# Two pairs of experts summed in PSUM before one eviction, with gather and sum moved around the transposes

## The chip, the cores and the metric

One core of a Trainium2 chip runs the whole program as a single launch. The metric is the device time in microseconds (us) of that launch; less is better. The core has TensorE (PE, with its weight loads PEld), VectorE (DVE), ScalarE (ACT), GpSimd (POOL) and the queue of SyncE (SP), from which most transfers out of device memory are issued. Each engine works through its own instructions in a fixed order and waits on semaphores for the others.

## What is computed

Two transformer blocks on 256 tokens of width 1024. The change lies in the second block, which has two layers. Each layer ends with a mixture of experts: 32 experts in 4 groups, of which every token uses the best two of its best group. In layer 0 there are 512 tokens (256 of the sequence and 256 of a context), in layer 1 only the 256 of the sequence. In short:

```python
def hier_moe(x, ...):
    g_idx = argmax(x @ w_group + b_group)            # group of a token, g_w its probability
    top_l, top_i = top_k(logits of that group, 2)
    top_w = softmax(top_l) * g_w
    expert = g_idx * 8 + top_i
    # every expert on the tokens that chose it
    hdn = silu(xb @ w_gate[e]) * (xb @ w_up[e])      # [n, 1024] -> [n, 512]
    ys = hdn @ w_down[e]                             # [n, 512] -> [n, 1024]
    return sum over a token's two experts of ys * top_w
h = h + gt2 * hier_moe(modulate(rms_norm(h)))
```

All inputs are float32. The weights of the 32 experts are 201 MB per layer (three matrices of 2 MiB per expert) and are read once.

## The kernel before

Everything of interest is in `moe(l, row, rt)`, which is run once per layer. Its slots give each expert 64 places for tokens (a rare expert with more tokens is treated after the loop). The loop `for P in range(16)` goes over pairs of experts, 2P and 2P + 1; four experts, so two pairs, are a quad `qd`.

- **Products of a pair.** `ex` computes gate, up and down for both experts of a pair side by side: expert i has 64 columns of the array, so that two matmuls of 64 columns run at the same time. Gate and up are 16 matmuls each (8 chunks of 128 features, 2 experts), down 16 (4 chunks, 2 halves of the output, 2 experts). They are float32, and each shows as two records in the trace. `next_tile` brings the weights in tiles of 1 MiB in the order of use, 12 per pair. The tiles go round seven places (four `raw`, three made of a `hi` and a `lo` buffer); six more tiles per layer, `early`, `rows` and `gt`, wait in other places from before the loop. So 13 tiles are loaded ahead, and later tiles are issued from SP as places come free.
- **Gather.** `gather(qd, kks)` fills `xq`, the features of the 4 x 64 slots of a quad, by matmuls with one-hot rows `oh` (line 1503), at 128 x 256. In layer 0 there are 64 per quad and half of them stand in each pair of the quad before. The one-hots are made by DVE inside `gather` (lines 1486 to 1493), at the place where the first half of the gather stands.
- **Combine.** `slots(P)` makes the one-hot `oht` and the weights of a pair on DVE. `y` is the pair's weighted output, split in two float32r parts by ACT (line 1600) and DVE (line 1601). `combine` turns it back to tokens: for each tile t of 128 tokens and each half n of the features, which I call a unit, two matmuls (line 1542) go into a PSUM buffer `tp`, DVE multiplies by the gate into `res` (line 1544, the eviction), and POOL adds `res` to `h` (line 1546; in the last pair DVE). Layer 0 has 8 units per pair, layer 1 has 4. There are three `tp` buffers, shared by gather, transposes and combine.
- **Transposes.** `sl = silu(gate) * up` (line 1572 on ACT, line 1578 on DVE) is transposed by four matmuls (line 1587), copied by ACT to `hT` (line 1589), and down follows.

In the text the combine of pair P - 1 stands around the product up of pair P, the gather ahead of the transposes. That is not the order on an engine: a scheduler at build time lays out each engine's instructions, by its own estimates, and may put them earlier. On PE, matmuls of combine are woven between those of gate and up.

Of the kernel before, what the change touches and what calls it, by code (L numbers as in the profile page):

```python
# [7 lines left out]
F32 = mybir.dt.float32  # L8
# [8 lines left out]
D = 1024  # L17
# [8 lines left out]
# ---------------------------------------------------------------------------  # L26
# constants that depend on shapes alone, packed in one [128, *] float32 array
# ---------------------------------------------------------------------------
# [10 lines left out]
def build_consts():  # L39
# [36 lines left out]
    # relative bias of the dilated mixer: bucket one-hot over m = t - s + 127  # L76
# [17 lines left out]
# units of background work (the modulation of the second block) emitted in the phases of the first block  # L94
# [6 lines left out]
def build(nc, tc, I, O, stop=""):  # L101
    """I: dict of input APs, O: output AP [256, 1024]."""
# [10 lines left out]
    @contextmanager  # L113
    def phase(name, nblk, nsm, nrow=1, nraw=0, ring=0):
        """Work memory of one phase: nblk blocks of 8 KB per partition, nsm of 2 KB, nrow of 4 KB; nraw more raw
        weight tiles; ring: further places in the order of the weight tiles."""
        with tc.tile_pool(name=name, bufs=1, reuse_waits="tile") as p:
            cur.update(pool=p, nblk=nblk, nsm=nsm, nrow=nrow, nraw=nraw, ring=ring, i=0)
            yield p
# [3 lines left out]
    def fill(n=1):  # L123
        """Emits n units of the background generators."""
        while n and bg:
            if next(bg[0], bg) is bg:
                bg.pop(0)
            else:
                n -= 1

    class Weave:
        """Spreads the units of generators over the slots of another loop."""
# [17 lines left out]
    def pipelined(n, stages, between=None):  # L150
        """stages[j](i) for items i < n, stage j of an item j steps after its first."""
# [11 lines left out]
    def blk(shape, dt=F32, name="blk", glob=False):  # L163
        """A block of the phase, or one that outlives it."""
# [84 lines left out]
    def load_exp(ap):  # L249
        """4 (or 2) k chunks of an expert's weight, also in buffers of split weights; k -> [128, width]."""  # L250
# [14 lines left out]
    class W:  # L265
        """Rows chunks of a weight tile as pairs (hi, lo)."""
# [29 lines left out]
    def rsqrt(ssq, n, inv_d):  # L296
        """(ssq * inv_d + eps) ** -0.5 for [128, n] sums of squares."""
# [12 lines left out]
    def rsqrt2(s0, s1, inv_d):  # L310
        """((s0 + s1) * inv_d + eps) ** -0.5 for two [128, 1] partial sums of squares."""
# [20 lines left out]
    def to_fm(src, nk, nt, xh, xl, gain=None, k0=0):  # L332
        """TM [128, nt, nk * 128] -> FM float32r pairs xh, xl [128, nk, nt * 128]; gain(k) -> [128, 1] column."""
# [22 lines left out]
    def row_rstd(hv, scr):  # L356
        """rms norm factor of the tokens of hv [128, D]; scr is overwritten."""
# [5 lines left out]
    def norm_tm(h, nt, rowv=None, glob=True):  # L363
        """h * rstd per token (* rowv), TM."""
# [28 lines left out]
    def token_order(kq, nt):  # L393
        """Order of (k, token tile) of a quad of k chunks: the last quad token by token."""
# [4 lines left out]
    class OutProj:  # L399
        """h += rms_norm(x @ w) * g; wtile(j) -> split pair [128, 2, 1024] of two k chunks."""  # L400
# [10 lines left out]
        def upto(self, xs, j1):  # L411
            """The k chunks below 2 * j1, the last pair of all token by token."""
# [30 lines left out]
    # ======================= first block =======================  # L443
    late = {}

    def rope_tables():
        SP.dma_start(consts[:, 128:], I["consts"][:, 128:CSPLIT])
        # rope tables of the positions: cos, sin [128, 2, 16]
# [29 lines left out]
    def setup():  # L478
        # conditions: silu(c), silu(c_ctx) as columns 4, 5; 32 columns from 4 - 2 c on have them at 2 c, 2 c + 1
# [11 lines left out]
        # lambda of both layers, on every partition  # L491
# [20 lines left out]
        # neighbourhood bias, rows (query row, head, key row), columns 63 - (kc - qc), in DRAM scratch  # L512
# [13 lines left out]
    def mla_layer():  # L526
        j = 0
        with phase("mla", 7, 7) as mp:
# [12 lines left out]
            # low-rank norms  # L541
# [27 lines left out]
            # q, TM, with rope on the last 32 of each 96  # L569
# [25 lines left out]
            # k (nope | rope) and v, TM  # L595
# [94 lines left out]
    def dil_bias():  # L690
        """Bias of the dilated heads over m = t - s + 127, to a DRAM scratch [48, 512]; loads first."""
# [14 lines left out]
    def dil_layer():  # L706
        with phase("dil", 5, 5) as mp:
# [8 lines left out]
            for qd in range(4):  # L716
# [24 lines left out]
                for hh in range(4):  # L741
# [3 lines left out]
                    # keys run backwards along the tile  # L745
# [47 lines left out]
    def ffn_layer(l):  # L793
        with phase(f"ffn{l}", 6, 8):
# [33 lines left out]
            # p @ ple_w_proj  # L828
# [33 lines left out]
    # ======================= second block =======================  # L862
# [5 lines left out]
    class Ada:  # L868
        """m = cond @ w_ada + b, row 32 j + 2 c + cond of [128, 512] for block 4 c + j, and as columns."""
# [32 lines left out]
        def cols(self, i):  # L902
            """[128, j2, b, cond] of parameter i."""
# [3 lines left out]
        def row(self, dst, i, cnd, n0, n1):  # L907
            """Halves n0 to n1 of parameter i on every partition."""
# [4 lines left out]
    def mixer(l, ada):  # L913
# [5 lines left out]
        # modulation columns g * (1 + scale), shift: [128, j2, b, cond]  # L919
# [7 lines left out]
        # x = modulate(rms_norm(h)), FM pairs, 4 k chunks of 512 tokens per block  # L927
# [24 lines left out]
        def proj_fm(c0, ntok, evac):  # L952
            """4 chunks of 128 columns from c0, FM over ntok tokens; evac(chunk, psum)."""
# [11 lines left out]
        def proj_tm(c0, ntile, evac):  # L965
            """512 columns from c0, TM; evac(t, psum)."""
# [28 lines left out]
        def transposed(p_sb, n, name):  # L995
            """[128 q, n * 128] -> [128 k, n * 128] blocks."""
# [13 lines left out]
        # keys, values, queries of the neighbourhood attention; halves of the spatial gating  # L1010
# [15 lines left out]
        def keys(t):  # L1026
            """First key and number of keys of a query tile."""
# [733 lines left out]
```

## Time and profile before

| | |
|---|---|
| timed runs | 3035.09, 3041.41, 3043.16 us, median 3041.41 |
| profiled execution | span 3046.4 us from the first to the last instruction; no other time is listed for it |
| PE busy | 2842.3 us, 93% of the span |
| DVE, ACT, POOL busy | 1383.3, 946.0, 384.1 us (45%, 31%, 13%) |
| transfers | 702.36 MB, on average 231 GB/s |
| expert loop of layer 0 (first product to last down) | 1599.7 to 2150.5 us |
| expert loop of layer 1 | 2548.1 to 3028.0 us |

The shares are averages over a program of many stages. PE is the busiest engine, but a PE that is "busy" may be at half clock, and the two expert loops have different limits, so they are read apart, by windows. In the timeline, rows of the same kind that follow one another are merged; the first number is the start, the second the length, and the bracket at the end is idle time with the engine that ended it. Matmuls overlap, so what one costs is read from start to start.

### The profile page before, as it was taken

Reading aid. Unit: us, or ns where it says so; the run is one execution under the profiler, and the core shown is the slowest. Engines: PE = TensorE matmul, PEld = TensorE weight load, DVE = VectorE, ACT = ScalarE, POOL = GpSimd, SP = SyncE. Lnnn points to the kernel's source line nnn. Section 1 sums busy time; section 2 is a strip of 40 time slices with the busy share of each in tenths; the row PEclk is TensorE's granted clock in tenths of the full one; section 3 lists DMA queues with packets and bytes.
Section 4 is the critical chain, followed back from the end, with each engine's and each line's share of the span. In section 5 each row is a group of like instructions: output and inputs, shape, how many; then the busy total and the mean of one; then the engine's idle time right before and its main releaser. Section 6 shows DMA issues by size and latency. Waiting matters only on the chain. (4 is left out here: it accounts for less than half of the span.)

```text
span 3046.4 us, 39455 instructions
## 1 busy us (share of the span) xinstructions
PE 2842.3 (93%) x15583; PEld 1972.6 (65%) x15583; DVE 1383.3 (45%) x2942; ACT 946.0 (31%) x1630; POOL 384.1 (13%) x304
## 2 busy tenths in 40 slices
PE   7999999998999999999979999999799997999996
PEld 6699789886997786678764444443486894333332
DVE  6555555445555426533472333333537564222222
ACT  5444444333444333433331001010334442111111
POOL 1010000000000201101031322223201001111111
PEclk9999999999999999999989999999899998999999
DMA  6665665665656432113468889889432386999997
GB/s 201 232 204 189 213 207 155 193 201 180 197 184 221 154 93 47 59 49 97 141 228 327 347 347 359 331 346 395 143 125 69 123 278 253 409 398 409 409 409 300
DMA packets 317148, 702.36 MB, mean 231 GB/s; under 512 B 36055, under 2 KB 179694, under 8 KB 310686
## 3 DMA queue, kind: packets, MB, share of 16 engines
q1 hardware_dynamic: 316622, 698.20, 64.0%
q8 instruction: 125, 2.05, 0.3%
q10 hardware_dynamic: 336, 1.59, 0.1%
q14 instruction: 65, 0.53, 0.0%
HBM read 697.91 MB, written 1.81 MB: 230 GB/s over the span
## 5 line engine op out<-in xcount | busy, mean ns | idle before, releaser
L280 DVE TENSOR_TENSOR lo<-raw,hi 128x1024 fp32r<-128x1024 f32 (+1 forms) x404 | 500.7, 1240 | 573.3 <-ACT hi L279 572.4
L279 ACT CAST hi<-raw 128x1024 fp32r<-128x1024 f32 (+1 forms) x418 | 433.7, 1039 | 623.4 <-PE mm L292 341.9
L291 PE MATMUL mm<-xh,hi 128*128 128x256 f32 (+1 forms) x1728 | 544.2, 316 | 3.7 <-ACT hi L279 2.5
L292 PE MATMUL mm<-xl,hi 128*128 128x256 f32 (+1 forms) x1728 | 538.3, 312 | 0.5 <-DVE xl L944 0.5
L293 PE MATMUL mm<-xh,lo 128*128 128x256 f32 (+1 forms) x1728 | 535.2, 310 | 1.2 <-POOL lo L280 1.2
L291 PEld LDWEIGHTS mm<-xh,hi 128*128 128x128 f32 x1728 | 333.4, 193 | 45.1 <-issue 20.3
L1532 PE MATMUL mm<-raw,xq 128*64 128x512 f32 x1152 | 345.3, 608 | 7.1 <-DMA raw<-in_moe_w_up_dram 3.9
L293 PEld LDWEIGHTS mm<-xh,lo 128*128 128x128 f32 x1728 | 333.0, 193 | 18.4 <-issue 1.8
L292 PEld LDWEIGHTS mm<-xl,hi 128*128 128x128 f32 x1728 | 333.5, 193 | 17.5 <-issue 2.0
L1546 POOL TENSOR_TENSOR h<-h,res 128x512 f32<-128x512 f32 x120 | 150.2, 1273 | 758.0 <-DVE res L1544 713.5
L1544 DVE TENSOR_TENSOR res<-tp,gt 128x512 f32<-128x512 f32 x192 | 123.0, 684 | 235.7 <-PE tp L1542 235.7
L1532 PEld LDWEIGHTS mm<-raw,xq 128*64 128x64 f32 x1152 | 100.0, 139 | 175.5 <-issue 156.6
L1601 DVE SCALAR_TENSOR_TENSOR y<-mm,wsum,y 128x512 fp32r<-128x512 f32 x64 | 47.1, 749 | 306.0 <-ACT y L1600 304.0
L291 PE MATMUL mm<-hi,xh 128*128 128x512 f32 (+2 forms) x504 | 174.9, 349 | 0.0
L293 PE MATMUL mm<-hi,xl 128*128 128x512 f32 (+2 forms) x504 | 174.9, 347 | 0.0
L292 PE MATMUL mm<-lo,xh 128*128 128x512 f32 (+2 forms) x504 | 174.4, 346 | 0.0
L1532 PE MATMUL mm<-raw,hT 128*64 128x512 f32 x568 | 160.1, 597 | 12.8 <-ACT hT L1589 12.6
L1532 PE MATMUL mm<-hi,xq 128*64 128x512 f32 x428 | 167.4, 603 | 0.6 <-DMA hi<-in_moe_w_up_dram 0.6
L1532 PE MATMUL mm<-lo,xq 128*64 128x512 f32 x428 | 159.7, 593 | 0.0
L1505 ACT COPY xq<-tp 128x512 f32<-128x512 f32 x64 | 37.5, 587 | 348.6 <-PE tp L1503 348.6
L280 POOL TENSOR_TENSOR lo<-raw,hi 128x1024 fp32r<-128x1024 f32 x14 | 33.7, 2422 | 861.2 <-ACT hi L279 766.0
L1542 PEld LDWEIGHTS tp<-y,oht 128*128 128x128 f32 x384 | 63.7, 188 | 119.3 <-issue 47.9
(486 smaller groups left out, 4588.3 us busy)
## 6 DMA issues: line engine op xcount, KB each, us to landing
raw<-in_moe_w_gate_dram SPq DMA_DIRECT2D x77, 1024.0 KB
raw<-in_moe_w_down_dram SPq DMA_DIRECT2D x71, 1024.0 KB
raw<-in_moe_w_up_dram SPq DMA_DIRECT2D x67, 1024.0 KB
raw<-in_w_in_dram SPq DMA_DIRECT2D x56, 1024.0 KB
raw<-in_w_ada_dram SPq DMA_DIRECT2D x48, 1024.0 KB
raw<-in_ffn_w_in_dram SPq DMA_DIRECT2D x44, 1024.0 KB
raw<-in_dil_w_qkv_dram SPq DMA_DIRECT2D x36, 1024.0 KB
hi<-in_moe_w_up_dram SPq DMA_DIRECT2D x59, 512.0 KB
```

What stands on the lines that cost most here:

```text
L279: A.copy(hv, rv[:, k0:k0 + n, :])
L280: (eng or V).tensor_tensor(lv, rv[:, k0:k0 + n, :], hv.bitcast(F32), op=ALU.subtract)
L291: T.matmul(ps, lhsT=lh, rhs=rh, start=first, stop=False)
L292: T.matmul(ps, lhsT=lh, rhs=rl, start=False, stop=False)
L293: T.matmul(ps, lhsT=ll, rhs=rh, start=False, stop=last)
L1505: A.copy(xq[:, 2 * kk:2 * kk + 2, :], p.rearrange("p (a b) -> p a b", b=256))
L1532: T.matmul(p[n][64 * i:64 * i + 64, :], lhsT=lhs(k, i), rhs=rv[i][kk][:, n * 512:(n + 1) * 512], start=k == 0, stop=k == kn - 1)
L1542: T.matmul(p, lhsT=oht[:, t * 128:(t + 1) * 128], rhs=y[:, i, ns], start=i == 0, stop=i == 1)
L1544: V.tensor_tensor(tmp, p, gts[:, t // 2, ns], op=ALU.mult)
L1546: (G if P < 15 else V).tensor_tensor(hs, hs, tmp, op=ALU.add)
L1601: V.scalar_tensor_tensor(y[:, 1, ns], py[n], wsum, y[:, 0, ns].bitcast(F32), op0=ALU.mult, op1=ALU.subtract)
```

## The change

- The one-hots of the gather get a function of their own, `onehots(qd)`, called in the even pair of a quad behind `slots`, instead of inside `gather`.
- `gather(qd + 1, ...)` moves wholly into the odd pair: two of its four parts ahead of the transposes, two behind them (between the transposes and down).
- `combine` now takes a list of two pairs (`done`), and sums four matmuls into one PSUM buffer per unit. It stands in the even pair alone: five eighths of the units ahead of the transposes, the rest behind them.
- `oht` of `slots` lies in a block of its own with four places, `ohts`, instead of one of the 2 KB buffers.
- In the last pair (P = 15), four units of the quad's first pair are begun before down, in three `tp` buffers and `po`; after the loop they are finished with the second pair's two matmuls, and other units get four matmuls in `mm` buffers. DVE adds these to `h`.

The core of the diff (comments and moved slices left out; line numbers of the changed file are about 20 to 40 higher, combine's matmul is line 1544, its eviction 1550, the gather's matmul 1505, products 1534, transposes 1604):

```diff
+        def onehots(qd):
+            dq = tiny.tile([128, nt, 2], F32, tag=f"dq{nt}", name="dq")
+            ...
+            state[qd] = (blk([128, 8, 256], name="xq", glob=True), oh)
         def gather(qd, kks):
-            if 0 in kks:
-                dq = tiny.tile([128, nt, 2], F32, tag=f"dq{nt}", name="dq")
-                ...
-                state[qd] = (blk([128, 8, 256], name="xq", glob=True), oh)
             xq, oh = state[qd]
 ...
-            oht = small(NT, F32R, name="oht")
+            oht = ohts[:, P % 4, :NT]
 ...
+        def summed(p, parts, t, n, first, last):
+            for j, (oht, y) in enumerate(parts):
+                for i in range(2):
+                    T.matmul(p, lhsT=oht[:, t * 128:(t + 1) * 128], rhs=y[:, i, ws_[n]], start=first and j + i == 0,
+                             stop=last and i == 1 and j == len(parts) - 1)
+        def added(p, t, n, eng):
+            tmp = small(name="res")
+            V.tensor_tensor(tmp, p, gts[:, t // 2, ws_[n]], op=ALU.mult)
+            hs = ht(t)[:, ws_[n]]
+            eng.tensor_tensor(hs, hs, tmp, op=ALU.add)
+        def combine(parts, us):
+            for t, n in us:
+                p = ps_tp()
+                summed(p, parts, t, n, True, True)
+                added(p, t, n, G)
 ...
             if P:
                 oht, wsum = slots(P)
-            if prev:
-                combine(*prev, range(nt // 2))
+            if not odd and qd < 7:
+                onehots(qd + 1)
             ex([pu], 8, xcols, 512)
             V.tensor_tensor(sl, sl, pu, op=ALU.mult)
 ...
-            if prev:
-                combine(*prev, range(nt // 2, nt))
-            if qd < 7:
-                gather(qd + 1, (0, 1) if P % 2 == 0 else (2, 3))
+            if odd:
+                if qd < 7:
+                    gather(qd + 1, (0, 1))
+            elif done:
+                combine(done, units[:cut])
             p = ps_tp()
             for b in range(4):
                 T.transpose(p[:, b * 128:(b + 1) * 128], sl[:, b * 128:(b + 1) * 128], ident)
             hT = small(name="hT")
             A.copy(hT, p)
+            if odd:
+                if qd < 7:
+                    gather(qd + 1, (2, 3))
+                else:
+                    for j, (t, n) in enumerate(units[:4]):
+                        open_.append(ps_tp() if j < 3 else ps_po())
+                        summed(open_[-1], now, t, n, True, False)
+            elif done:
+                combine(done, units[cut:])
             py = [ps_mm(), ps_mm()]
             ex(py, 4, lambda k, i: hT[:, k * 128 + i * 64:k * 128 + i * 64 + 64], 1024)
 ...
-            prev = (P, oht, y)
-        combine(*prev, range(nt))
+            now.append((oht, y))
+            if odd:
+                done, now = now, []
+        for j, (t, n) in enumerate(units):
+            if j < 4:
+                summed(open_[j], done[1:], t, n, False, True)
+                added(open_[j], t, n, V)
+            else:
+                p = ps_mm()
+                summed(p, done, t, n, True, True)
+                added(p, t, n, V)
```

What the scheduler makes of it is seen at three places of layer 0. In these rows `xq` stands for products gate and up, `hT` for down, `y,oht` (later `y,ohts`) for combine, `oh` for gather, and `consts,silu` for the transposes; what comes ahead of an arrow's comma list as `raw`, `hi` or `lo` is the weight tile.

DVE in the even pair P = 2, from the pair's `oht` on. Before:

```order
L1518 SCALAR_TENSOR_TENSOR oht<-rows,sid,o1t 128x512
L1544 TENSOR_TENSOR res<-tp,gt_13680 128x512 x4
L1510 TENSOR_SCALAR sid<-consts 128x1
L1578 TENSOR_TENSOR silu<-silu,mm 128x512
L1544 TENSOR_TENSOR res<-tp,gt_13680 128x512 x4
L1492 TENSOR_SCALAR o_14334<-consts,dq 128x256
L1492 TENSOR_SCALAR o_14337<-consts,dq 128x256
L1493 SCALAR_TENSOR_TENSOR oh<-consts,dq,o_14334 128x256
L1493 SCALAR_TENSOR_TENSOR oh<-consts,dq,o_14337 128x256
```

After:

```order
L1520 SCALAR_TENSOR_TENSOR ohts<-rows,sid,o1t 128x512
L1492 SCALAR_TENSOR_TENSOR oh<-consts,dq,o_14212 128x256
L1491 TENSOR_SCALAR o_14215<-consts,dq 128x256
L1491 TENSOR_SCALAR o_14218<-consts,dq 128x256
L1492 SCALAR_TENSOR_TENSOR oh<-consts,dq,o_14215 128x256
L1492 SCALAR_TENSOR_TENSOR oh<-consts,dq,o_14218 128x256
L1550 TENSOR_TENSOR res<-tp,gt_13680 128x512 x3
```

The one-hots stood behind the eight evictions of the pair; now they stand in front of all of them.

PE in pair P = 4, from its first combine to its transposes. Before (these rows are followed by the last six products and by 32 matmuls of the gather):

```order
L1542 MATMUL tp<-y,oht 128x512 x6
L1532 MATMUL mm<-raw,xq 64x512 x16
L1532 MATMUL mm<-hi,xq 64x512 x4
L1532 MATMUL mm<-lo,xq 64x512
L1542 MATMUL tp<-y,oht 128x512 x2
L1532 MATMUL mm<-lo,xq 64x512 x3
L1542 MATMUL tp<-y,oht 128x512
L1532 MATMUL mm<-hi,xq 64x512
L1542 MATMUL tp<-y,oht 128x512 x7
L1532 MATMUL mm<-raw,xq 64x512
```

After:

```order
L1544 MATMUL tp<-y,ohts 128x512 x4
L1534 MATMUL mm<-raw,xq 64x512
L1544 MATMUL tp<-y,ohts 128x512 x8
L1534 MATMUL mm<-raw,xq 64x512 x15
L1534 MATMUL mm<-hi,xq 64x512 x4
L1534 MATMUL mm<-lo,xq 64x512 x4
L1534 MATMUL mm<-hi,xq 64x512
L1544 MATMUL tp<-y,ohts 128x512 x8
```

The combine of the even pair now goes over two pairs, in fewer and longer runs; there is still a run of one matmul of the products (the second row).

PE around the transposes. Before (P = 4), they come behind the gather and directly before down:

```order
L1503 MATMUL tp<-oh,xlo 128x256
L1503 MATMUL tp<-oh,xhi 128x256
L1503 MATMUL tp<-oh,xlo 128x256
L1503 MATMUL tp<-oh,xhi 128x256
L1503 MATMUL tp<-oh,xlo 128x256
L1587 MATMUL tp<-consts,silu 128x128 x4
L1532 MATMUL mm<-raw,hT 64x512 x9
```

After (P = 4):

```order
L1534 MATMUL mm<-raw,xq 64x512
L1534 MATMUL mm<-lo,xq 64x512
L1534 MATMUL mm<-raw,xq 64x512
L1534 MATMUL mm<-lo,xq 64x512
L1534 MATMUL mm<-raw,xq 64x512
L1604 MATMUL tp<-consts,silu 128x128 x4
L1544 MATMUL tp<-y,ohts 128x512 x12
L1534 MATMUL mm<-raw,hT 64x512 x9
```

Now the last product of up stands directly before the transposes, and combine (in odd pairs gather) between the transposes and down.

## Rows read from the trace of the kernel before

**Rows 1.** Windows of the two expert loops; the first line names the columns

```profile
core 0: us, PE busy (x) PEld busy (x) DVE busy (x) ACT busy (x) POOL busy (x), PEclk, DMA share, GB/s
...
1599.70:2150.50 550.80, 514.78 (x2289) 222.27 (x2288) 182.13 (x349) 56.83 (x94) 150.49 (x120) 0.98 0.89 345
...
2548.10:3028.00 479.90, 443.73 (x1945) 172.87 (x1944) 115.58 (x258) 57.63 (x94) 75.10 (x60) 1.00 0.99 392
```

**Rows 2.** Waits of PE in layer 0's loop: us in total, times, longest us

```profile
PE tp L1503 <- DVE oh L1493: 16.8, 8, 4.7
PE mm L1532 <- ACT hT L1589: 12.6, 16, 1.1
PE tp L1542 <- ACT y L1600: 3.2, 4, 0.8
PE tp L1587 <- DVE silu L1578: 1.7, 2, 0.9
PE tp L1542 <- DVE y L1601: 1.4, 5, 0.3
```

**Rows 3.** Waits of PE in layer 1's loop

```profile
PE tp L1587 <- DVE silu L1578: 8.8, 11, 0.9
...
PE mm L1532 <- DMA raw<-in_moe_w_up_dram: 3.9, 5, 1.5
PE mm L1532 <- DMA raw<-in_moe_w_gate_dram: 3.2, 3, 1.5
```

**Rows 4.** Window inside layer 1's loop

```profile
2725.00:2750.00 25.00, 23.42 (x106) 8.91 (x108) 5.57 (x10) 2.36 (x4) 5.01 (x4) 1.00 1.03 409
```

**Rows 5.** Timeline of DVE, end of the even pair P = 8

```profile
1893.57 2.32 DVE L1492 TENSOR_SCALAR o<-consts,dq 128x256 f32<-128x256 f32 x2
```

**Rows 6.** Windows of layer 0's loop at half clock: one of five, and their sum

```profile
1820.10:1826.90 6.80, 6.02 (x14) 2.00 (x15) 2.44 (x7) 0.00 (x0) 0.18 (x1) 0.50 0.55 218
...
sum 27.20, PE 24.34 PEld 16.19 DVE 10.35 ACT 0.53 POOL 1.33; mean PE 4.87 PEld 3.24 DVE 2.07 ACT 0.11 POOL 0.27
```

**Rows 7.** Timeline of PE in pair P = 14, around the transposes

```profile
2107.67 1.89 PE L1532 MATMUL mm<-raw,xq 128*64 128x512 f32 x8
2110.44 0.66 PE L1587 MATMUL tp<-consts,silu 128*128 128x128 f32 x4 [0.89 <-DVE silu L1578]
2111.83 1.52 PE L1532 MATMUL mm<-raw,hT 128*64 128x512 f32 x6 [0.73 <-ACT hT L1589]
```

**Rows 8.** Timeline of PE in pairs P = 7 and 8, pieces

```profile
1854.50 2.32 PE L1542 MATMUL tp<-y,oht 128*128 128x512 f32 x8
1856.75 1.07 PE L1532 MATMUL mm<-raw,xq 128*64 128x512 f32 x2
...
1874.74 1.07 PE L1542 MATMUL tp<-y,oht 128*128 128x512 f32 x2 [0.82 <-ACT y L1600]
...
1880.49 4.46 PE L1532 MATMUL mm<-raw,xq 128*64 128x512 f32 x20
1884.78 0.59 PE L1532 MATMUL mm<-hi,xq 128*64 128x512 f32 x1
...
1886.08 0.59 PE L1532 MATMUL mm<-raw,xq 128*64 128x512 f32 x1
1886.60 0.74 PE L1542 MATMUL tp<-y,oht 128*128 128x512 f32 x2
1887.27 0.64 PE L1532 MATMUL mm<-lo,xq 128*64 128x512 f32 x1
...
1889.12 0.51 PE L1542 MATMUL tp<-y,oht 128*128 128x512 f32 x1
1889.56 1.07 PE L1532 MATMUL mm<-hi,xq 128*64 128x512 f32 x2
1890.56 2.08 PE L1542 MATMUL tp<-y,oht 128*128 128x512 f32 x7
```

**Rows 9.** Group of evictions on DVE in layer 0's loop: busy us, mean ns, idle before

```profile
L1544 DVE TENSOR_TENSOR res<-tp,gt 128x512 f32<-128x512 f32 x120 | 76.6, 684 | 127.0 <-PE tp L1542 127.0
```

More of the change, by code (lines that the diff above doesn't have):

```diff
@@ L1479, in moe @@
         state = {}
-        def gather(qd, kks):
-            nonlocal noh
-            if 0 in kks:
-                dq = tiny.tile([128, nt, 2], F32, tag=f"dq{nt}", name="dq")
-                V.tensor_scalar(dq, d12, -256.0 * qd, None, op0=ALU.add)
-                oh = []
-                for t in range(nt):
-                    o1 = small(256, name="o1")
-                    o2 = ohs[:, noh % (nt + 1)]
-                    noh += 1
-                    V.tensor_scalar(o1, iota, dq[:, t, 0:1], None, op0=ALU.is_equal)
-                    V.scalar_tensor_tensor(o2, iota, dq[:, t, 1:2], o1, op0=ALU.is_equal, op1=ALU.add)
-                    oh.append(o2)
-                state[qd] = (blk([128, 8, 256], name="xq", glob=True), oh)
+        def onehots(qd):
+            nonlocal noh
+            dq = tiny.tile([128, nt, 2], F32, tag=f"dq{nt}", name="dq")
+            V.tensor_scalar(dq, d12, -256.0 * qd, None, op0=ALU.add)
+            oh = []
+            for t in range(nt):
+                o1 = small(256, name="o1")
+                o2 = ohs[:, noh % (nt + 1)]
+                noh += 1
+                V.tensor_scalar(o1, iota, dq[:, t, 0:1], None, op0=ALU.is_equal)
+                V.scalar_tensor_tensor(o2, iota, dq[:, t, 1:2], o1, op0=ALU.is_equal, op1=ALU.add)
+                oh.append(o2)
+            state[qd] = (blk([128, 8, 256], name="xq", glob=True), oh)
+        def gather(qd, kks):
             xq, oh = state[qd]
@@ L1533, in ex @@
                                      rhs=rv[i][kk][:, n * 512:(n + 1) * 512], start=k == 0, stop=k == kn - 1)
-        def combine(P, oht, y, ts):
-            for t in ts:
-                for n in range(2):
-                    ns = slice(n * 512, n * 512 + 512)
-                    p = ps_tp()
-                    for i in range(2):
-                        T.matmul(p, lhsT=oht[:, t * 128:(t + 1) * 128], rhs=y[:, i, ns], start=i == 0, stop=i == 1)
-                    tmp = small(name="res")
-                    V.tensor_tensor(tmp, p, gts[:, t // 2, ns], op=ALU.mult)
-                    hs = ht(t)[:, ns]
-                    (G if P < 15 else V).tensor_tensor(hs, hs, tmp, op=ALU.add)
+        units = [(t, n) for t in range(nt) for n in range(2)]
+        ws_ = slice(0, 512), slice(512, 1024)
+        def summed(p, parts, t, n, first, last):
[13 more added lines that the diff above has]
+                added(p, t, n, G)
+        onehots(0)
         gather(0, range(4))
@@ L1559, in moe @@
         A.dma_start(drows, tkT[:4 * nt])
-        prev = None
+        cut = 5 * len(units) // 8
+        done, now, open_ = [], [], []
         for P in range(16):
-            qd = P // 2
+            qd, odd = divmod(P, 2)
             xq = state[qd][0]
             def xcols(k, i):
-                c = (P % 2 * 2 + i) * 64
+                c = (odd * 2 + i) * 64
                 return xq[:, k, c:c + 64]
@@ L1595, in moe @@
                     row(gts[:, u], 5, u, 0, 2)
+                ohts = blk([128, 4, 512], F32R, name="ohts")
                 oht, wsum = slots(P)
@@ L1598, in moe @@
             for n in range(2):
-                ns = slice(n * 512, n * 512 + 512)
-                A.activation(y[:, 0, ns], py[n], AF.Copy, scale=wsum)
-                V.scalar_tensor_tensor(y[:, 1, ns], py[n], wsum, y[:, 0, ns].bitcast(F32), op0=ALU.mult,
+                A.activation(y[:, 0, ws_[n]], py[n], AF.Copy, scale=wsum)
+                V.scalar_tensor_tensor(y[:, 1, ws_[n]], py[n], wsum, y[:, 0, ws_[n]].bitcast(F32), op0=ALU.mult,
                                        op1=ALU.subtract)
-            prev = (P, oht, y)
-        combine(*prev, range(nt))
+            now.append((oht, y))
[9 more added lines that the diff above has]
+                added(p, t, n, V)
         ecnt = tiny.tile([128, 1], F32, tag="ecnt", name="ecnt", bufs=1)
```

## The prediction

> **What bounds the kernel now.** I read the windows of the two expert loops first, since only their instructions change. The loop of layer 0 takes 550.8 us, with PE busy for 514.8 of them and the transfers at a share of 0.89 and 345 GB/s. The loop of layer 1 takes 479.9 us with the transfers at 0.99 [rows 1]. Inside it most windows of 25 us read like that of [rows 4], 409 GB/s at a share of 1.03, so that is the most that the transfers give. Then I read who ended PE's waits. In layer 0 no transfer is among them: PE waits for DVE and ACT alone [rows 2]. In layer 1 PE waits for weights too [rows 3]. So layer 0 is bound by PE, layer 1 by the transfers, and what the change saves on PE counts in layer 0 alone. A bound for how much: 179 tiles of 1.05 MB (192 less the 13 that are loaded ahead) at 409 GB/s take 459 us. Layer 0 could lose some 70 to 90 us before its transfers end it, layer 1 (459 of 479.9) next to nothing.
>
> **The change, part by part, in layer 0.** The counts of matmuls of products, gather and transposes stay, and combine's too: two pairs by two matmuls per unit are as many as before. What changes is what stands between them.
>
> *One-hots.* PE waits 16.8 us, eight times, for the one-hots of the gather [rows 2], all of it in even pairs. The cause is seen on DVE: they are made behind the pair's evictions, right when the gather wants them, the first two at 1.2 us each [rows 5]. Now they stand in front of the evictions, and the gather's first matmul stands some 20 us later, in down of the even pair or in the odd pair. What covers them is the product up; the wait goes. **-16.8 us** (no reason for a rest: at worst the two shortest waits stay, 1 to 2 us).
>
> *Clock.* After these waits TensorE runs at the lower of its two levels, 1.2 GHz: five stretches, 27.2 us in all, with PE busy for 24.3 of them [rows 6]. Half of that is lost, 12 us. Without the waits ahead of them the stretches should go: **-12 us**, with 0 as the other bound, should other waits bring them back (a rival below).
>
> *Transposes.* Down waits for `hT` in each of 16 pairs, 12.6 us [rows 2]. Gather or combine now stands there (12 matmuls or more, over 2 us), so this goes. But the order after shows a new wait. Ahead of the transposes the scheduler has moved gather and combine away, into up and even in front of it: in 12 of 16 pairs the last product stands directly before the transposes, in two more only half a unit is between, in two enough. In that place PE waits for `silu * up`. Before, it did so in the last two pairs alone (1.7 us) [rows 2], and there it is 0.89 us [rows 7]; in layer 1 eleven times, 8.8 us [rows 3]. So I put 12 x 0.87 + 2 x 0.4 = 11 us against 12.6 + 1.7: **-3 us**. Bounds: -14 if the fillers cover it after all, +3 if the half units cover nothing and DVE is late.
>
> *Wait for y.* Combine waits for the newest `y`, 3.2 + 1.4 us [rows 2]. It is now only met in the even pairs, and there the older pair's two matmuls come first. In four pairs it stands directly behind down. A wait of 0.8 us [rows 8] less those two matmuls' 0.2 us gives 0.6 for each: **-2 us** (0 to -4).
>
> *Lone halves.* Two products share the array, one for each expert: 20 records, so 5 pairs of matmuls, from 1880.49 to 1884.78, take 0.86 us for each pair. A single one takes as long: at 1889.56 one matmul (two records) stands between two pieces of combine, and the next starts 1.00 us later [rows 8]. So every run of products with an odd number wastes half a slot, and two such runs a slot of 0.86 us. I counted them in the order of PE: before, the 15 pairs with combine hold 26 such extra slots (pair 4: runs of 21, 3, 1, 7, so 2 extra); after, 16 (pair 4: 1, 24, 7, so 1). **-8.6 us**. The bounds are the count's, -7 to -9.
>
> *Changes of shape.* From the last product to combine takes 0.52 us instead of 0.43, and two matmuls of combine and the way back to products 0.67, a single one 0.44 [rows 8]. So one more matmul costs 0.23, and an excursion with two some 0.3 us more than its matmuls, of which I give 0.1 to the unit (next item) and 0.2 to leaving and coming back. In the order, PE leaves the products 79 times before (67 for combine, 10 for gather, 2 for transposes) and 61 times after (29, 20, 12). 18 x 0.2 = **-3.6 us** (-2 to -5).
>
> *Fewer evictions.* Eight matmuls of combine in a row take 2.25 us, 0.28 each [rows 8], against the 0.23 just found. I put the rest, 0.1 us per two, at the start of a unit, where the matmul waits for a free buffer or its semaphore. 120 units become 59: **-6 us** (0 to -8). DVE's evictions, 76.6 us for 120 [rows 9], and POOL's adds halve as well. Neither engine ends the loop (182 and 150 of 550.8 us busy [rows 1]), so this is worth nothing by itself; and with four matmuls, some 1.0 us, per eviction of 0.68 us, three buffers are enough.
>
> *New waits elsewhere.* In even pairs DVE has `oht` and one-hots, some 7 us, in front of the first evictions. Queued behind them are three full `tp` buffers; combine's next unit comes only after a run of 24 products, over 10 us later, so the cover holds. If it were gone, 3 us for each of 7 quads would be lost. The end of the layer has the same eight evictions and adds on DVE; PE's eight more matmuls there lie beside them. I put **0 to +1 us**.
>
> *Transfers.* The sum so far is -52 us: 499 us, or 31.2 us per pair of experts. The transfers of a pair (12 tiles of 1.05 MB at 409 GB/s) take 30.8. That is nearly even, and 13 tiles are ahead at the start, so the transfers should not end the loop, but single waits can come where gate, up and down follow each other closely. **+2 us**; the upper bound is the rate of such waits in layer 1 when they come, 0.8 us each [rows 3] in 16 pairs: +13.
>
> **Layer 1.** The same edits save some 20 us on PE, and the transfers keep all but what lies before they are full: **-1 us** (-8 to +3). Everything else in the program keeps its order.
>
> **Sum.** -52 + 1 + 2 - 1 = -50 us. Against the profiled execution's span that is 3046.4 - 50 = 2996; the timed runs' median, 3041.4, is 5 us below that span, so **2991 us**, 1.6% faster. Both ends of the terms together: the best (no wait for `silu * up`, -11 more, and -7 more in layer 1) gives 2972; the worst (transfers +11 more, clock half kept +6, transposes +6, evictions nothing +6, rounded down because they won't all come) gives 3014.
>
> **Rivals.**
> *A: the transfers take over in layer 0.* For it: 30.8 against 31.2 us per pair, and a share of 0.89 at the present pace. Against: the loop of layer 1 shows 409 GB/s kept up with the same seven places. One wait of 0.8 us per pair: 3004 us.
> *B: nothing to gain, since the loop of layer 0 is bound by the transfers already.* Then 3038 to 3045. Against: no wait for a transfer in [rows 2].
> *C: slower, by the clock.* In nearly each pair PE now stands idle 0.9 us before the transposes. If each such place brought a stretch at 1.2 GHz like the one of 6.8 us in [rows 6], each pair would lose 3.4 us. In layer 0 that is 54 us, which eats the gain whole; in layer 1, where PE has little more than 2 us per pair to spare with the edits, some 20 us more: 3041 - 50 + 54 + 20 = 3065. It decides from about 15 of the 32 pairs on. Against: before, layer 1 has eleven of these waits (8.8 us), each followed by the transposes and by the wait for `hT`, and its granted clock is 1.00 [rows 1, 3]; the wait at 2110 us, with 0.89 and 0.73 us on either side of the transposes [rows 7], is not among the five stretches either. The Trainium skill speaks for it: "TensorE: Matmul & The Clock Gate", Part 4: PE-mode transpose, states that a transpose doesn't bring TensorE to its upper level as a matmul does. By that rule idle time and transposes would go together, and the time would be this rival's; the trace does not agree, with 1.00 in layer 1.
> *D: the cover of the evictions in even pairs is too short.* 7 x 3 = 21 us: 3012. Against: 10 us of products stand there.
>
> **How the numbers follow.** The forecast (2980 to 3000) has 0.72, A 0.14, B 0.04, C 0.05, D 0.05. Forecast, A and D are faster by more than 0.3% (about what a measurement of this kernel can tell from no change): 0.91. B is the same: 0.04. C is slower: 0.05. The range of 8 in 10 is 2972 to 3014, the bounds of the terms; it takes in A and D.
>
> **What would show it.** Right: the loop of layer 0 ends some 50 us earlier, at about 500 us; among PE's waits there, that for `oh` and that for `hT` are gone, and a wait for `silu` of about 0.87 us stands 12 times; the stretches at half clock are gone but for one or two; units of combine are 60; the loop of layer 1 is within 3 us of 480. Wrong: waits for transfers of more than 10 us in layer 0 (A), a granted clock below 0.96 in either loop (C), waits of combine for `res` (D), or a change of more than 5 us outside layer 0's loop.

## The result, and the profile after

The median went from 3042.28 us (3035.09 to 3046.35) to 2995.24 us (2989.14 to 2998.15), four runs of each: a ratio of 0.9846, with a 95% interval from 0.983 to 0.9862. The forecast was 2991 us in a range of 2972 to 3014. The profiled executions read here have spans of 3046.4 and 2993.4 us, so they differ by 53 us where the medians differ by 47; the former is above its median.

Windows of the two expert loops after, from the first product to the last down, with the columns of [rows 1]:

```profile
core 0: us, PE busy (x) PEld busy (x) DVE busy (x) ACT busy (x) POOL busy (x), PEclk, DMA share, GB/s
1596.60:2099.90 503.30, 492.02 (x2286) 216.56 (x2286) 133.39 (x286) 57.75 (x95) 71.03 (x56) 1.00 0.96 378
2500.00:2975.30 475.30, 439.59 (x1943) 175.31 (x1937) 90.31 (x225) 55.93 (x92) 35.29 (x28) 1.00 1.00 396
```

Against [rows 1], the loop of layer 0 lost 47.5 us and that of layer 1 4.6; all the rest together lost 0.9. The granted clock of layer 0's loop is 1.00 instead of 0.98, so the five stretches at 1.2 GHz [rows 6] are gone. POOL has half its work. In layer 1 the share of the transfers was 0.99 already, which is why the same edits gave a tenth there.

Waits of PE in layer 0's loop after (us in total, times, longest); these two rows are all there is, and answer to the five of [rows 2]:

```profile
PE tp L1604 <- DVE silu L1594: 11.0, 14, 1.2
PE po L1544 <- DVE y L1628: 0.3, 1, 0.3
```

The waits for `oh` and `hT` are gone; the new one, for `silu * up`, is there 14 times. In layer 1's loop transfers are what PE waits for most, against 3.9 and 3.2 us in [rows 3]:

```profile
PE mm L1534 <- DMA raw<-in_moe_w_up_dram: 17.3, 11, 2.7
PE tp L1604 <- DVE silu L1594: 13.1, 15, 1.2
PE mm L1534 <- DMA hi<-in_moe_w_up_dram: 3.5, 5, 1.5
PE mm L1534 <- DMA raw<-in_moe_w_gate_dram: 0.8, 1, 0.8
```

DVE in the even pair P = 8 after; it answers to [rows 5]:

```profile
1851.78 0.87 DVE L1492 SCALAR_TENSOR_TENSOR oh<-consts,dq,o 128x256 fp32r<-128x256 f32 x2
1852.58 1.88 DVE L1550 TENSOR_TENSOR res<-tp,gt 128x512 f32<-128x512 f32 x3
...
1861.44 0.69 DVE L1550 TENSOR_TENSOR res<-tp,gt 128x512 f32<-128x512 f32 x1 [6.92 <-PE tp L1544]
```

The last one-hot is done at 1852.65, in front of the evictions. The gather's first matmul in this pair starts at 1873.68, 21 us later.

PE in down of the same pair after:

```profile
1870.09 3.66 PE L1534 MATMUL mm<-raw,hT 128*64 128x512 f32 x16
1873.68 0.39 PE L1505 MATMUL tp<-oh,xhi 128*128 128x256 f32 x1
...
1874.71 1.93 PE L1534 MATMUL mm<-raw,hT 128*64 128x512 f32 x4
1876.57 0.39 PE L1505 MATMUL tp<-oh,xlo 128*128 128x256 f32 x1
```

The first run, eight matmuls, takes 3.59 us from start to start: four slots of 0.86 us and the change of shape. The second has an even number too, two, and takes 1.86 us: two slots. Both of its matmuls are of the same expert, so of the same 64 columns of the array, while the other 64 have nothing to do. That row shows what the prediction got wrong (below).

### The profile page after: what moved, and what is told of

It reads as the page before. It is cut to its first block, busy times and chain, and to the rows that moved or that the text cites. A ratio compares the mean times of both kernels' runs of the same rounds, so it can differ in the third digit from the quotient of the medians.

```text
span 2993.4 us, 39143 instructions
## 1 busy us (share of the span) xinstructions
PE 2815.5 (94%) x15583; PEld 1969.2 (66%) x15583; DVE 1304.0 (44%) x2846; ACT 944.5 (32%) x1630; POOL 264.7 (9%) x208
## 5 line engine op out<-in xcount | busy, mean ns | idle before, releaser
L1534 PE MATMUL mm<-raw,xq 128*64 128x512 f32 x1152 | 334.4, 598 | 18.1 <-DMA raw<-in_moe_w_up_dram 17.3
L292 PEld LDWEIGHTS mm<-xl,hi 128*128 128x128 f32 x1728 | 332.9, 193 | 17.7 <-issue 2.0
L1534 PE MATMUL mm<-raw,hT 128*64 128x512 f32 x568 | 181.3, 599 | 0.0
L1594 DVE TENSOR_TENSOR silu<-silu,mm 128x512 f32<-128x512 f32 x32 | 22.0, 688 | 347.9 <-PE mm L1534 347.9
L1552 POOL TENSOR_TENSOR h<-h,res 128x512 f32<-128x512 f32 x56 | 71.4, 1295 | 800.4 <-DVE res L1550 793.7
L1627 ACT ACTIVATE y<-mm,wsum 128x512 fp32r<-128x512 f32 x64 | 43.7, 689 | 279.8 <-PE mm L1534 269.8
L1534 PEld LDWEIGHTS mm<-raw,hT 128*64 128x64 f32 x568 | 53.1, 136 | 87.7 <-issue 83.8
```

Source lines behind the costliest of these rows:

```text
L292: T.matmul(ps, lhsT=lh, rhs=rl, start=False, stop=False)
L1534: T.matmul(p[n][64 * i:64 * i + 64, :], lhsT=lhs(k, i), rhs=rv[i][kk][:, n * 512:(n + 1) * 512], start=k == 0, stop=k == kn - 1)
L1552: eng.tensor_tensor(hs, hs, tmp, op=ALU.add)
L1594: V.tensor_tensor(sl, sl, pu, op=ALU.mult)
L1627: A.activation(y[:, 0, ws_[n]], py[n], AF.Copy, scale=wsum)
```

## Experiments

Theory: most of the gain is the wait for the one-hots and the half clock behind it, and PE's order sets most of the rest. Rivals: halving the evictions and adds is what pays; or moving the gather around the transposes. All times of loops are from the first product to the last down, 550.8 us before and 503.3 after. A slot is the 0.86 us of two matmuls of 64 columns side by side, or of one alone; a run of products is what stands between two changes of shape. Both are counted in the order of PE in layer 0's loop.

**The one-hots alone** (`e1_onehots_early`). The kernel before, with `onehots(qd)` cut out of `gather` as in the change, and only its call moved:

```diff
             if P:
                 oht, wsum = slots(P)
+            if P % 2 == 0 and qd < 7:
+                onehots(qd + 1)
             if prev:
                 combine(*prev, range(nt // 2))
```

> The kernel before with one edit of the change: the one-hots of the gather are made in the even pair directly behind slots, ahead of the evictions on DVE. Combine, evictions, adds and the place of the gather stay as before. Theory (the waits for the one-hots and the half clock behind them are most of the gain): PE's wait for oh, 16.8 us before, falls under 2 us; the five stretches at half clock (27.2 us) go; the order of PE also has 3 lone half slots and 7 runs of products fewer, some -4 us. Loop of layer 0 from 550.4 to 516 to 521 us, layer 1 within 2 us, total near 3009 us, ratio 0.989. Rival (the summing in PSUM with its halved evictions and adds is what pays): less than 10 us gained, loop of layer 0 above 540 us.

Median 3008.16 us, ratio 0.9894 (0.9877 to 0.991). PE's waits in layer 0, and the window of the loop:

```profile
PE mm L1533 <- ACT hT L1593: 11.7, 16, 0.8
PE tp L1543 <- ACT y L1604: 3.3, 4, 0.8
PE tp L1591 <- DVE silu L1582: 1.7, 2, 0.9
PE tp L1543 <- DVE y L1605: 1.4, 5, 0.3
...
1597.20:2112.50 515.30, 496.91 (x2289) 214.88 (x2289) 170.27 (x349) 56.74 (x94) 150.33 (x120) 1.00 0.95 369
```

No wait for `oh` and a clock of 1.00, with all 120 evictions and adds in place (POOL 150 us). 35 of the 47.5 us come with this edit alone, most of them by the waits (16.8) and the half clock: the rival, under 10 us, falls.

**The sum alone** (`e2_sum_only`). The changed kernel, with gather and one-hots put back:

```diff
-            if not odd and qd < 7:
-                onehots(qd + 1)
 ...
+            if not odd and done:
+                combine(done, units[:cut])
+            if qd < 7:
+                if not odd:
+                    onehots(qd + 1)
+                gather(qd + 1, (2, 3) if odd else (0, 1))
```

> The kernel with the sum over two pairs in PSUM (60 units of combine instead of 120) and its combine in the even pair, but the gather in its old places, half in each pair behind combine, and the one-hots made there, behind five of the eight evictions on DVE. Lone half slots by the order 41 (before 36), places with the transposes behind the last product 8 (before 2), none with down directly behind the transposes (before 16). Theory (the gain comes from the one-hots' place, and the sum by itself is worth a few us): the wait for oh stays at some 8 us or more with half clock behind it; 550.9 - 12.6 (hT) - 4 (y) - 5 (units) - 1 (runs) + 6 (silu) + 4 (halves) - 10 (part of oh and clock) = 528, range 520 to 541 us. Rival (the sum and its halved evictions are the gain): wait for oh gone and 515 us or less.

3010.94 us in one run. Layer 0's loop takes 517.0 us, just under the range of the theory and above the rival's:

```profile
PE tp L1603 <- DVE silu L1592: 6.8, 8, 0.9
PE tp L1505 <- DVE oh L1492: 3.7, 5, 2.7
PE po L1544 <- DVE y L1624: 0.3, 1, 0.3
```

I had expected 8 us or more of waits for `oh`. Only 3.7 are left: ahead of the one-hots there are now five evictions instead of eight, made earlier, and one stretch at half clock (3.4 us) instead of five. The even pair still has eight evictions; three of them stand behind `silu * up`. So this run shows what the place of the evictions in DVE's queue does. That their halved number does it is not shown: no run has fewer evictions with all of them still in front of the one-hots. Each of the two parts by itself takes away most of the wait for the one-hots. The loop loses 35 and 34 us, and the gain of both, 47.5, is far from the sum. The 34 hold more than the one-hots: the waits for `hT` (12.6) are gone too and those for y are down by 4.3, while those for `silu` grow by 5.1 and 11 more slots are lost to lone halves (9.4 us, counted below).

**The one-hots late, but in the odd pair** (`e3_onehots_in_gather`). The changed kernel with this move:

```diff
-            if not odd and qd < 7:
-                onehots(qd + 1)
 ...
             if odd:
                 if qd < 7:
+                    onehots(qd + 1)
                     gather(qd + 1, (0, 1))
```

> The changed kernel with the one-hots made inside the gather again, so in the odd pair instead of the even one. In the odd pair DVE has no evictions of combine any more. Theory (the one-hots were late because they stood behind eight evictions in the same pair): the wait for oh stays away, under 3 us, no stretch at half clock, loop of layer 0 502 to 506 us; so moving the combine out of the gather's pair would have done the same. Rival (they must be made a pair ahead): the wait for oh comes back with 10 us or more and brings half clock with it, loop of layer 0 515 to 532 us.

2989.97 us in one run, loop of layer 0 498.0 us, clock 1.00:

```profile
PE tp L1603 <- DVE silu L1592: 10.2, 12, 0.9
PE mm L1534 <- ACT hT L1605: 0.7, 1, 0.7
PE po L1544 <- DVE y L1627: 0.3, 1, 0.3
```

There is no wait for `oh`. So being a pair early is not needed; it is enough that no evictions stand in front of the one-hots. The loop is even 5 us shorter than that of the changed kernel, with an order on PE that leaves fewer column halves idle (below).

**Two evictions per unit again** (`e9_two_evictions`). The changed kernel with:

```diff
-                p = ps_tp()
-                summed(p, parts, t, n, True, True)
-                added(p, t, n, G)
+                for part in parts:
+                    p = ps_tp()
+                    summed(p, [part], t, n, True, True)
+                    added(p, t, n, G)
```

> The changed kernel, but combine evicts the part of each pair by itself: two matmuls, one eviction, one add, so 120 units of combine in layer 0 as before instead of 60; nothing else of the text is changed. In the order on PE this gives 3 lone half slots more, 8 runs more, 3 places fewer where the transposes follow the last product. Theory (an eviction by itself is off the path, a unit's start costs 0.1 us): +2.6 + 1.6 - 3 + 5.7 = +7 us, loop of layer 0 506 to 512 us. Rival (the sum in PSUM pays by itself, since evictions and adds load DVE and POOL): 520 us or more, with PE waiting for res or tp.

3001.31 us in one run, loop of layer 0 511.8 us, +8.5:

```profile
PE tp L1605 <- DVE silu L1595: 8.3, 11, 0.9
PE po L1544 <- ACT y L1628: 0.8, 1, 0.8
PE po L1544 <- DVE y L1629: 0.3, 1, 0.3
```

No wait for `tp` or `res`. So the sum in PSUM by itself is worth some 5 to 9 us, mostly on PE, as the theory said, and not through DVE's or POOL's load.

**The gather moved** (`e6_gather_moved`). The kernel of the first experiment, and:

```diff
-            if qd < 7:
-                gather(qd + 1, (0, 1) if P % 2 == 0 else (2, 3))
+            if qd < 7 and P % 2:
+                gather(qd + 1, (0, 1))
 ...
             A.copy(hT, p)
+            if qd < 7 and P % 2:
+                gather(qd + 1, (2, 3))
```

> The kernel before (combine per pair, 120 units) with the one-hots made early in the even pair and the gather moved wholly into the odd pair, two parts on either side of the transposes. Compared with the kernel that has the early one-hots alone (loop of layer 0 515.4 us): down stands directly behind the transposes in 9 places instead of 16, 3 to 4 more places have the last product in front of them, 2 lone half slots fewer, 2 runs more. Theory (a wait for hT is 0.8 us, a wait for silu 1.03, a lone half slot 0.86): -5.6 + 3.5 - 1.7 + 0.4 = -3 us, 510 to 514 us. Rival (moving the gather around the transposes is worth the whole wait for hT or more): 503 us or less.

3007.18 us in one run, loop of layer 0 510.3 us against 515.3:

```profile
PE mm L1533 <- ACT hT L1593: 6.6, 9, 0.8
PE tp L1591 <- DVE silu L1582: 4.5, 6, 0.9
```

As expected: the wait for `hT` falls by 5.1 us and that for `silu` rises by 2.8, so more than half of what the gather covers behind the transposes is taken back in front of them. The waits for y, not expected to change, fall by 1.4 us; the rest of the 5 us is not split up.

**PE in the order of the text** (`e4_pinned`, `e5_before_pinned`). Each matmul of the expert loop is held behind the one before it in the text, in the changed kernel and in the kernel before:

```diff
+        def keep(f):
+            def g(*x, **k):
+                return tc.keep_in_program_order(f(*x, **k))
+            return g
 ...
-                            T.matmul(p[n][64 * i:64 * i + 64, :], lhsT=lhs(k, i),
+                            keep(T.matmul)(p[n][64 * i:64 * i + 64, :], lhsT=lhs(k, i),
```

and so on for gather, combine and transposes.

> The changed kernel with the matmuls of the expert loop held in the order of the text on PE (products, then combine or gather, transposes, combine or gather, down). No product stands alone then: lone half slots 33 to 0, runs of products 68 to 32, places where the transposes follow the last product 12 to 2. Theory (a lone column half costs a full slot of 0.86 us, a change of shape 0.2 us, such a place 1.03 us): PE needs 28 + 7 + 10 = 45 us less in layer 0, 457 us. The transfers (179 tiles at 409 GB/s are 459 us, and layer 1 with that rate takes 476) then end the loop, so 475 to 482 us, with waits for weights of 10 us or more on PE; layer 1 within 3 us; total near 2970 us, ratio to the kernel before 0.976. Rival (a lone half costs nothing much, since my count of them moved by 3 slots only): 502.7 - 7 - 10 = 485 us and no waits for weights. Rival (the woven order is worth something, since it covers waits for y and buffers): 503 us or more.

> The kernel before with the matmuls of the expert loop held in the order of the text on PE, nothing else. Lone half slots 36 to 0 (-31 us), runs of products 86 to 47 (-8), wait for silu before the transposes in no pair (-1.7). The one-hots are still made behind eight evictions and the gather stands directly behind the last combine, now in all seven even pairs. Theory (the prices hold, and the wait for the one-hots grows from 16.8 us to some 4 us in each of 7 quads, with 12 to 17 us for half clock): loop of layer 0 515 to 530 us; total near 3017, ratio 0.992. Rival (lone halves cost little): 540 us or more. Rival (the terms simply add): 510 us.

The changed kernel in this order has a median of 2975.33 us, ratio 0.9784 (0.9767 to 0.98), the shortest of the kernels that load all their weights. Its loop of layer 0 takes 485.5 us, and its waits there now read like those of layer 1:

```profile
PE mm L1498 <- DMA raw<-in_moe_w_up_dram: 16.5, 14, 2.2
PE tp L1498 <- DVE silu L1599: 1.7, 2, 0.9
...
1596.10:2081.60 485.50, 465.80 (x2285) 218.19 (x2284) 133.77 (x287) 57.97 (x94) 69.87 (x56) 1.00 0.99 392
```

The transfers end both loops (layer 1 475.1 us). The expected 475 to 482 us was missed by 3: no stretch of 31 us in this loop moves more than 410 GB/s, and the first moves only 316.

The kernel before in this order stays nearly where it was, 3037.07 us, ratio 0.9982 (0.997 to 0.9995). Its loop of layer 0 falls to 527.9 us, as expected, but PE now waits this long for the one-hots, at a clock of 0.97:

```profile
PE tp L1483 <- DVE oh L1498: 28.0, 6, 4.7
PE mm L1483 <- ACT hT L1594: 11.9, 16, 0.8
...
1597.50:2125.40 527.90, 485.54 (x2291) 224.20 (x2289) 185.67 (x350) 57.45 (x94) 150.14 (x120) 0.97 0.92 360
```

In layer 1 there are now 21.3 us of the same waits (2.0 before) and a clock of 0.95; the loop is 16 us longer (495.8), which I had not put down: the total is 20 us above what I expected. An order that helps the changed kernel by 20 us gives 4 to the kernel before, since there the woven order covers some of the one-hots.

**The order of the text with half of the loads** (`e8_pinned_half_loads`). In layer 0, from the third pair on, every second tile is taken twice instead of loading the next:

```diff
             ntile += 1
+            if l == 0 and ntile % 2 == 0 and ntile > 24:
+                return state["w"]
-            return tiles.pop(ntile - 1, None) or load_exp(exp_ap(ntile - 1))
+            state["w"] = tiles.pop(ntile - 1, None) or load_exp(exp_ap(ntile - 1))
+            return state["w"]
```

> The changed kernel with PE held in the order of the text, and in layer 0, from the third pair of experts on, every second weight tile is not loaded: the tile before it is used again, so the products of those tiles are wrong and half of the transfers of the loop are left out. Against the run in the order of the text with all loads (loop of layer 0 485.6 us, 17 us of waits for weights on PE, transfers at a share near 1.02) this tells what the transfers took there. Theory (in that order the transfers end the loop, and PE by itself needs 457 us: the changed kernel's 503.3 less 28 for lone halves, 7 for changes of shape, 10 for waits for silu): 455 to 463 us and no wait for weights. Rival (the lone halves cost less than a full slot, so PE needs 480 us or more by itself): 478 to 486 us.

2942.41 us in one run. Loop of layer 0:

```profile
1597.70:2049.00 451.30, 448.90 (x2279) 212.35 (x2275) 132.69 (x283) 57.23 (x93) 69.80 (x56) 1.00 0.63 226
```

There is no wait for a weight. So PE by itself needs 451.3 us in that order, 52 less than the changed kernel takes, and the transfers took 34 of it back in the run with all loads. Only half of the 34 shows there as waits for weights; PE counts as busy for the rest (465.8 against 448.9 us). The order that the scheduler chose costs the changed kernel 52 us of PE, not the 45 that my prices gave.

**Halves tile by tile** (`e11_halves_by_tile`). The prices so far assumed that a column half runs beside its neighbour in the order or not at all. This run asks for that alone:

```diff
-                for kk in range(per):
-                    k = kq * per + kk
-                    for n in range(width // 512):
-                        for i in range(2):
+                for i in range(2):
+                    for kk in range(per):
+                        k = kq * per + kk
+                        for n in range(width // 512):
```

> The changed kernel with PE in the order of the text and one more edit: the products take a whole weight tile of the first expert, then the whole tile of the second, so four matmuls of one column half come in a row (AAAABBBB) instead of turn by turn (ABABABAB). The same matmuls, loads and sums. It prices a column half that has no neighbour of the other half. Counted by the rule that two neighbours share a slot if and only if they are of different halves, gate and up take 25 slots instead of 16 and down 13 instead of 8: 14 slots more in each of 16 pairs. Theory (each costs a full slot of 0.857 us): 192 us more than the 451.3 us that PE needs in the order of the text with half of the loads; the transfers (30.8 us per pair) are hidden behind 40 us of PE: loop of layer 0 635 to 650 us, layer 1 some 620 us or more, total 3250 to 3300. Rival (PE lets a matmul pass the three before it, or a half by itself is cheaper): below 560 us; if it is free, 486 us as in the order of the text with all loads.

2996.11 us in one run, loop of layer 0 497.0 us. The theory, 635 to 650, falls by far. The run of down in pair P = 3 shows why (`raw` is the first expert's tile here, `hi` and then `lo` the second's; each matmul has two records):

```profile
1712.86 2.36 PE L1498 MATMUL mm<-raw,hT 128*64 128x512 f32 x5
1714.63 0.64 PE L1498 MATMUL mm<-hi,hT 128*64 128x512 f32 x1
1715.06 0.59 PE L1498 MATMUL mm<-raw,hT 128*64 128x512 f32 x1
1715.11 0.59 PE L1498 MATMUL mm<-hi,hT 128*64 128x512 f32 x1
1715.48 0.59 PE L1498 MATMUL mm<-raw,hT 128*64 128x512 f32 x1
```

The second expert's first record starts at 1714.63, ahead of the last three of the first expert's eight, which stand before it in the order. From there on both halves work side by side, each 0.43 us per record. What can't be made good is the difference: if one half has more matmuls than the other before PE changes to another shape, the rest run alone. By this rule a run takes as many slots of 0.86 us as its busier half has matmuls. The changed kernel's runs bear it out. From its first record to the next shape, a run of down in the order ABABABABAABBABAB takes 7.07 us (8 slots by this rule are 6.86, the 9 of neighbours 7.71), ABABABABAA 5.29 (6 slots are 5.14; 5, if nothing were lost, 4.29), AA 1.86 (2 slots are 1.71). All 49 runs of layer 0 that end at gather or combine take 0.14 to 0.21 us more than their slots, and in none do more than two of one half stand in a row. With four in a row the order does cost something: the loop takes 45.7 us more than the 451.3 above, though both halves have the same number in each of its 17 runs. Each of the 14 that end at gather or combine takes at least 2.3 us more than the slots and the 0.21; late weights that don't show as waits may be a part of the rest. The counts of 33, 36 and 41 in the expectations above are by the rule that fell; by this one the lost slots are 26 before, 29 after, 22 with the one-hots alone, 37 with the sum alone, 25 with the one-hots in the odd pair, 23 with the gather moved, 32 with two evictions, and 0 in the order of the text.

## Why the prediction was right, and where it was not

**One-hots, -16.8, and clock, -12: shown.** Both rows are gone after, and the first experiment takes both away with one edit. Its 35 us are these 29 and, by the prices below, 4 lost slots (3.4) and 6 runs (2.3) fewer. The 12 of the clock is the prediction's estimate and was not measured by itself. The prediction gave both to the one-hots' new place; the second experiment shows that the sum, with its combine's new place, would have removed most of the wait alone.

**Transposes, -3: shown.** 14.3 us of waits for `hT` and `silu` [rows 2] became 11.0, at the 14 places that were read in the order, with the sum of 11 us forecast.

**Wait for y, -2: measured -4.3** (4.6 to 0.3). By the order, the older pair's two matmuls or products stand ahead of it now; that they are what covers it was not tried by itself.

**Lone halves, -8.6 with bounds of -7 to -9: the step that failed.** It put half a slot on every run of products with an odd number and counted 26 slots before and 16 after. The numbers of odd runs are right, but an even run can lose as much: in down, the changed kernel's order puts pieces of the gather or of combine behind two matmuls of the same expert, as in the row at 1874.71 above. 13 even runs lose a slot each, so 29 are lost after, not 16: 3 x 0.86 = +2.6 us, a loss outside the bounds. What had to be counted was the difference between the experts in each run.

**Changes of shape, -3.6: too small, by what is left over.** Of the 52 us between the changed kernel and the order of the text on PE alone, the halves are 29 x 0.86 = 25, the waits for `silu` 9.3; 62 runs of products, counted in the trace, became 17, so the 17.7 us left are 0.39 us for each of 45, if all of them are put there. [Rows 8] give nearly that: one matmul of products takes 1.00 us to combine, 0.14 more than its slot, and a single one of combine 0.44 back to products, 0.21 more than its 0.23, together 0.35. The prediction gave a part of this to the units. Its 18 fewer runs are then -6 to -7. The Trainium skill says in "TensorEngine Tiling (Array Packing)", Tiling Modes, that the tiles of one mode work independently and that changing the mode drains TensorE. The trace agrees with both: a half runs three records ahead within a run, and what it has left over stands alone at the run's end. The page states no time; from a product to gather or combine it is 0.52 us here, where 0.43 is the products' own pace.

**Fewer evictions, -6: near.** The run with two evictions lost 8.5 us: 2.6 for halves and 7 x 0.39 = 2.7 for runs, -2.7 for `silu`, +0.8 for y, and so 5.1 for 56 units, 0.09 for each against 0.1 forecast.

**Transfers, +2 in layer 0, and -1 in layer 1.** Layer 0 had no wait for them; layer 1 gave 4.6 us. Rival A was not far: 18 us of PE's time less, and the transfers end layer 0's loop too (485.5 us).

**The sum.** With the measured sizes: -16.8 - 12 - 3.3 - 4.3 + 2.6 - 7 - 5 = -45.8 us of the 47.5 that layer 0 lost; 1.7 us have no owner. The waits are measured; the clock is the prediction's estimate, and halves, shape and evictions are counts times the prices above. The total was right since the 11.2 us that the halves were off were made good, for the most part by shape (3.4), y (2.3), transfers (2) and layer 1 (3.6), all of them off in the other direction. No run ties these errors to each other, so that they cancel is luck.

**Rivals.** B, C and D didn't come: no wait for `tp` or `res`, and clocks of 1.00 in both loops, with PE idle some 0.8 us and then transposing in 29 of 32 pairs. On rival C, the rule on transposes in the Trainium skill ("TensorE: Matmul & The Clock Gate", Part 4: PE-mode transpose) has no effect to be seen here; the stretches at 1.2 GHz in these loops go with the waits for `oh` (last section).

## What to carry to other kernels

When two edits are offered for one gain, ask of each which wait it removes: here either of them takes away most of the wait for the one-hots, and the second adds 12 to 14 us where it would give 34 or 35 alone. Where two matmuls share the array by columns, count for each stretch between changes of shape how many belong to each half; the surplus is lost. The order within the stretch cost nothing with up to two of a half in a row, and up to 46 us in 17 stretches with four. A scheduler's weave is worth reading for its price: held in the order of the text, the changed kernel's PE needs 10% less for the loop (451.3 against 503.3 us), and then the transfers are the bound (485.5).

## What the runs showed of the hardware

- Matmuls on different column halves are not tied to their neighbour: with four of each half in a row, the second half started ahead of three records (1.3 us) of the first that stood before it. Of 192 us that strict order would have cost, at most 46 were lost (497.0 against 451.3 us).
- A matmul of 64 columns with nothing on the other half takes 0.86 us, the same as two side by side.
- What went ahead of half clock in layer 0's loop: each of the eleven waits of 2.7 to 4.7 us for `oh` (four in the kernel before, six in its order of the text, one with the sum alone) has 3.4 or 6.8 us at 1.2 GHz with it; two waits of 1.1 and 0.4 us close together had 3.4 us once and none the other time; the 14 waits of up to 1.2 us before the transposes after had none.
